# Four more 4 KB tiles in the general pool, and a smaller scratch for dynamic DMAs

## The chip, the core and the metric

The kernel runs on one NeuronCore of a Trainium2 chip. The metric is the device time of one execution in microseconds, lower is better; a run's time covers the profiled span of the core (first to last instruction) and a few microseconds around it.

## What is computed

One layer of an encoder on 2048 tokens of width 1024, all in float32:

```
xn  = rmsnorm(x, norm_mix)
u   = xn @ w_in                       # q 512, k 512, v 1024, o 1024, gates 16
h   = mlstm_scan(q,k,v,gates) forward + the same backward   # 16 chunks of 128 tokens, 4 heads
h   = headnorm(h) * head_norm * sigmoid(o)
x   = x + h @ w_out
x   = x + square(relu(rmsnorm(x, norm_mlp) @ w1)) @ w2      # w1 1024x4096, w2 4096x1024
x   = x + sigmoid(rmsnorm(x, norm_ple) @ ple_gate_w + b) * (p @ ple_w)
out = rmsnorm(x, norm_final)
```

The scan carries a matrix state per head from chunk to chunk, so chunks run in sequence; everything else is matrix products on token blocks.

## The kernel before, in words

Each float32 operand of a product is split into a high part and a remainder, both of a rounded float32 type, and each product of two operands becomes three matmuls (high by high, high by low, low by high; `mm3`, L186 to L189). So in front of TensorE stands a constant stream of splits: ScalarE writes the high part (`A.copy`), VectorE subtracts to get the low part (`split`, L165 to L167). The big projections (k, q and o of the second half of the tokens, w1, w2) are done with a seven-product scheme on 2x2 blocks (`SEVEN`, L418): blocks are added and subtracted first (`sa`, `ta`, `T1` to `T4`), then split (`op`), then multiplied.

The stages, in order of time:

- up to about 270 us: norm of x, the v projection of the second half, then seven-product jobs for k, q and o;
- to about 540 us: v, k, q and o of the first half, with the backward scan woven in (`bwd_steps`, L806: load v and k of a chunk, split them, update the state, store it to `cb_d`);
- to about 900 us: the forward scan over 16 chunks (`Chunk`, L943), with `w_out` and the start of the MLP's input;
- to about 1520 us: the product with w1 for two blocks of tokens (`up_job`, L1264), results stored to `hid_d`;
- to about 2150 us: the product with w2 (`down_job`, L1292); hidden values come back by `hst` loads (L1111, L1116), weights by `wst` loads (L1128), sums go out as accumulating DMAs (L1297);
- to the end: the gate stage, token tile by token tile (`Tok`, L1372). Tokens are transposed by a round trip through memory: `Early_h.put` (L1357) writes eight DMAs of 128 KB each from GpSimd, `Early_h.get` (L1365) reads them back.

**Memory.** Nearly all tiles of the kernel come from one general pool: `Ht` (L74) makes a tile with tag `H`, and all tiles of that tag share `NH` slots, each as large as the largest tile of the tag (4128 bytes a partition for the state tiles with 4 x 258 floats; most tiles are 4096). Staged weights, split weights, transposed tokens, block sums, split operands, hidden values, the scan's tiles: all are `H`. Two smaller pools stand beside it: `O` (`NO` = 7 slots) for loads that are read early, and `S` (6 slots of 2 KB) for results on the way out. The instruction that first writes a tile has to wait until all readers of the slot's last tile are done; if that instruction is a load, the whole DMA queue of SyncE waits behind it, and if it is a split, its engine does.

**Order.** Up to L1504 the order on VectorE, ScalarE and TensorE is the order of the program text (`strict`). After that the framework's planner sets the order of each queue when the program is built: it simulates the kernel with its own costs and lets each engine take the earliest instruction of the program text whose inputs and slot are free at that moment. On the chip the queues then run in that fixed order. So the number of slots enters twice: in waits on the chip, and in the order that the planner writes down.

**DMAs.** SyncE issues most loads and many stores (hardware descriptors); GpSimd issues 408 DMAs whose descriptors are written by software into the scratch for dynamic DMAs, which lies at the bottom of every partition of the on-chip memory, 16384 bytes of it by default. The framework gives the DMAs of GpSimd eight completion counters in turn, so a ninth one waits until the first of the last eight has landed.

The lines that set the sizes:

```
NH = 39
NO = 7
def Ht(name, shape, dt=F32):
    return sb.tile(shape, dt, tag="H", bufs=NH, name=name)
```

Of the kernel before, what the change touches and what calls it, by code (L numbers as in the profile page):

```python
# [26 lines left out]
DFF = 4096  # L27
PLE = 256
EPS = 1e-6
NH = 39  # L30
NO = 7
QC, KC, VC, OC, GC = 0, 512, 1024, 2048, 3072

# [2 lines left out]
def hybrid_mlstm_kernel(  # L36
# [37 lines left out]
    def Ht(name, shape, dt=F32):  # L74

        return sb.tile(shape, dt, tag="H", bufs=NH, name=name)

# [1670 lines left out]
```

## Time and profile before

| | |
|---|---|
| time, median of 3 runs | 2401.54 us (2399.94 to 2401.57) |
| span of the profiled execution | 2396.9 us |
| median of the runs less that span | 4.6 us |
| TensorE busy | 2359.8 us (98%) |
| VectorE, ScalarE, GpSimd busy | 1564.8, 1164.3, 629.9 us |
| DMA | 441.18 MB, mean 184 GB/s |
| largest DMA issues | `wst<-in_mlp_w` 96 of 512 KB, 5.2 us to landing; `h_d<-o` 96 of 512 KB, 13.4 us |

The profile holds one execution. Its own time outside the span is not recorded, so it is compared with the runs through the 4.6 us between span and median. Of the profile's views the following are used: the page, the table of busy time by stretches, who waited for whom, the chain of work, and the time line of one engine.

### The profile page before, as it was taken

The numbers are of one execution on the slowest core, as the hardware profiler recorded it, in microseconds if no ns is written. First come the engines' busy times: TensorE is split into PE (matmuls) and PEld (weight loads), VectorE is DVE, ScalarE is ACT, GpSimd is POOL, SyncE is SP. The second block draws the span as 40 slices with busy tenths as digits, with TensorE's granted clock in tenths as the row PEclk, the third lists the DMA queues.
The fourth block names the chain that finished last, engine by engine and source line by source line (L and its number), as shares of the span: only waits on it lengthen the run. The fifth ranks groups of instructions, "written<-read, shape, count | busy, mean of one in ns | idle before, by whom it ended". The sixth has DMA issues, their size and how long they took to land.

```text
span 2396.9 us, 31578 instructions
## 1 busy us (share of the span) xinstructions
PE 2359.8 (98%) x11221; PEld 1949.9 (81%) x11221; DVE 1564.8 (65%) x2611; ACT 1164.3 (49%) x2166; POOL 629.9 (26%) x679
## 2 busy tenths in 40 slices
PE   7999999999999999999999999999999999999998
PEld 6988888788889887888888888787888888888886
DVE  6677545557778887666685544767666667666665
ACT  5234434437788874343353333444444444455554
POOL 0041122124333324446533332011111111111121
PEclk9999999999999999999999999999999999999999
DMA  5676656868668883456663332568686776796453
GB/s 177 228 225 196 192 144 224 281 220 295 230 227 296 277 269 110 132 169 209 215 228 106 106 114 71 176 134 196 142 189 164 170 170 153 173 216 178 136 138 87
DMA packets 274038, 441.18 MB, mean 184 GB/s; under 512 B 48936, under 2 KB 182440, under 8 KB 273880
## 3 DMA queue, kind: packets, MB, share of 16 engines
q1 hardware_dynamic: 211608, 309.00, 39.3%
q0 software_dynamic: 61984, 129.64, 23.2%
q8 instruction: 88, 1.44, 0.2%
q14 instruction: 70, 0.57, 0.1%
q10 hardware_dynamic: 288, 0.52, 0.1%
HBM read 263.39 MB, written 175.50 MB: 183 GB/s over the span
## 4 chain that ended last, share of the span: by engine, by line
PE 91%; DVE 4%; ACT 2%; issue 1%; DMA 1%; POOL 0%; DVEq 0%; ACTq 0%; SPq 0%; POOLq 0%
PE pa L100 33%; PE pb L100 16%; PE pc L100 8%; PE pg L100 7%; PE psf L100 7%; PE psv L100 7%; PE pso L100 5%; PE pn L100 2%; PE pl L100 2%; PE pu L100 2%; PE pt L100 1%; DVE op L100 1%; PE pS L100 0%; ACT jk L100 0%; DMA wst<-in_mlp_w 0%
## 5 line engine op out<-in xcount | busy, mean ns | idle before, releaser
L100 PE MATMUL pa<-op 128*128 128x512 f32 x3360 | 824.2, 394 | 3.6 <-ACT e L100 2.1
L100 PEld LDWEIGHTS pa<-op 128*128 128x128 f32 x3360 | 629.5, 188 | 155.7 <-ACT e L100 4.4
L100 PE MATMUL pb<-op 128*128 128x512 f32 x1632 | 407.7, 394 | 0.8 <-DVE op L100 0.8
L100 PEld LDWEIGHTS pb<-op 128*128 128x128 f32 x1632 | 306.2, 188 | 73.8 <-DVE op L100 1.1
L100 DVE TENSOR_TENSOR op<-sa,op 128x1024 fp32r<-128x1024 f32 (+2 forms) x176 | 189.1, 1080 | 143.3 <-ACT op L100 109.7
L100 ACT CAST op<-sa 128x1024 fp32r<-128x1024 f32 (+2 forms) x176 | 156.6, 894 | 189.7 <-PE pb L100 98.1
L1297 POOL DMA_DIRECT2D h_d<-o x96 | 94.8, 1033 | 529.9 <-DVE o L100 443.7
L100 ACT COPY e<-pa 128x512 f32<-128x512 f32 x160 | 93.7, 586 | 278.4 <-PE pa L100 277.9
L100 PE MATMUL pc<-op 128*128 128x512 f32 x768 | 191.9, 394 | 0.1
L100 PEld LDWEIGHTS pc<-op 128*128 128x128 f32 x768 | 144.1, 188 | 34.6 <-DVE op L100 0.6
L100 PE MATMUL psv<-whi,xT 128*128 128x272 f32 (+2 forms) x720 | 161.1, 317 | 0.6 <-DVE xT L98 0.6
L100 PE MATMUL psf<-xT,whi 128*128 128x512 f32 x512 | 160.9, 395 | 0.0
L100 ACT CAST op<-wst 128x512 fp32r<-128x512 f32 x112 | 92.5, 834 | 113.9 <-DVE op L100 59.8
L100 DVE TENSOR_TENSOR op<-wst,op 128x512 fp32r<-128x512 f32 x112 | 122.8, 1099 | 30.8 <-ACT op L100 18.5
L467 POOL TENSOR_TENSOR sa<-wst 128x512 f32<-128x512 f32 x32 | 58.8, 1838 | 262.2 <-PE pb L100 167.3
L100 PEld LDWEIGHTS psv<-whi,xT 128*128 128x128 f32 x720 | 118.6, 188 | 9.8 <-DVE xT L98 0.8
L100 PE MATMUL psv<-wlo,xT 128*128 128x272 f32 (+2 forms) x360 | 113.8, 316 | 0.0
L100 PEld LDWEIGHTS psf<-xT,whi 128*128 128x128 f32 x512 | 95.4, 188 | 21.3
L100 DVE TENSOR_TENSOR op<-hst,op 128x384 fp32r<-128x384 f32 (+1 forms) x96 | 65.5, 688 | 64.7 <-ACT op L100 45.1
L100 PE MATMUL pso<-whi,hThi 128*128 128x512 f32 x256 | 102.0, 399 | 2.6 <-ACT nt L100 1.4
L100 PE MATMUL pg<-whi,xTh 128*128 128x512 f32 x256 | 101.4, 397 | 0.0
L100 PE MATMUL psf<-xT,wlo 128*128 128x512 f32 x256 | 100.9, 394 | 0.0
(261 smaller groups left out, 4371.4 us busy)
## 6 DMA issues: line engine op xcount, KB each, us to landing
wst<-in_mlp_w SPq DMA_DIRECT2D x96, 512.0 KB, 5.2
h_d<-o POOLq DMA_DIRECT2D x96, 512.0 KB, 13.4
hid_d<-e SPq DMA_DIRECT2D x128, 256.0 KB, 2.5
hst<-hid_d SPq DMA_DIRECT2D x64, 384.0 KB, 6.8
wst<-in_mlstm_w_in SPq DMA_DIRECT2D x44, 512.0 KB, 5.2
vst<-v_d SPq DMA_DIRECT2D x31, 512.0 KB, 4.7
raw<-in_x SPq DMA_DIRECT2D x16, 512.0 KB, 6.6
kq<-kq_d SPq DMA_DIRECT2D x16, 512.0 KB, 4.0
```

Source lines behind the costliest of these rows:

```text
L100: r = f(*a, **kw)
L467: eng.tensor_tensor(s[:, 0], r1[:, :, P:], r2[:, :, P:], op=add_)
L1297: G.dma_start(rows(h1_d, 2 * q + i), o[i], accum_op=add_)
```

## The change

Two numbers. The pool's slots go from 39 to 43, for all tiles with the tag `H` at once, in every stage; and the scratch for software descriptors goes from the default 16384 to 4096 bytes a partition. Four slots of 4128 bytes are 16512 bytes; 12288 come from the scratch and the rest from bytes that no tile used. No instruction is added or taken out.

```diff
-NH = 39
+NH = 43
 NO = 7
...
-    nc = _bacc.Bacc("TRN2", target_bir_lowering=False, num_devices=1)
+    nc = _bacc.Bacc("TRN2", target_bir_lowering=False, num_devices=1, dynamic_dma_scratch_size=4096)
```

## The prediction, made before the result was known

> **What bounds the kernel now.** First the table of the cores, for the span and the mean granted clock, then the busy time of each engine on the page.
>
> ```profile
> core 0: 2396.9 us, clock 0.997
> ```
>
> ```profile
> PE 2359.8 (98%) x11221; PEld 1949.9 (81%) x11221; DVE 1564.8 (65%) x2611; ACT 1164.3 (49%) x2166; POOL 629.9 (26%) x679
> ```
>
> TensorE is idle for 2396.9 - 2359.8 = 37.1 us of the span, at nearly the full granted clock. More memory removes no matmul, so it can only shorten this idle time. Next, where it lies: the table of busy time by stretches of 60 us (window, PE busy and its count, then PEld, DVE, ACT, POOL, clock, DMA share, GB/s), and below it the first and the last matmul from the time line of TensorE.
>
> ```profile
> 0.00:60.00 60.00, 47.63 (x222) 37.22 (x223) 37.63 (x74) 32.16 (x63) 0.83 (x7) 1.00 0.54 177
> 420.00:480.00 60.00, 57.46 (x272) 47.76 (x271) 33.10 (x77) 24.95 (x43) 11.54 (x18) 0.97 0.86 283
> 540.00:600.00 60.00, 56.78 (x309) 48.07 (x308) 43.49 (x75) 42.16 (x104) 29.11 (x31) 1.00 0.81 291
> 600.00:660.00 60.00, 58.34 (x352) 50.86 (x351) 45.66 (x100) 46.57 (x131) 20.41 (x29) 1.00 0.69 234
> 840.00:900.00 60.00, 58.92 (x330) 50.70 (x328) 48.32 (x90) 44.65 (x114) 14.53 (x17) 1.00 0.79 263
> 900.00:960.00 60.00, 57.92 (x248) 46.21 (x247) 45.59 (x45) 27.07 (x34) 28.55 (x12) 1.00 0.34 110
> 1320.00:1380.00 60.00, 60.00 (x261) 48.58 (x260) 29.28 (x31) 20.25 (x28) 20.52 (x14) 1.00 0.36 114
> 1500.00:1560.00 60.00, 59.06 (x251) 46.53 (x250) 42.89 (x72) 28.62 (x48) 5.99 (x6) 1.00 0.59 183
> 1620.00:1680.00 60.00, 59.17 (x254) 47.29 (x253) 42.89 (x69) 28.28 (x45) 7.29 (x8) 1.00 0.78 188
> ```
>
> ```profile
> 8.65 0.45 PE L100 MATMUL pt<-ident,xs 128*128 128x128 f32 x1 [8.65 <-DVE xs L98]
> ```
>
> ```profile
> 2385.08 0.40 PE L100 MATMUL pl<-whi,pTl 128*128 128x512 f32 x1
> ```
>
> The first stretch lacks 60 - 47.63 = 12.4 us: 8.65 before the first matmul, the rest in the ramp, whose order is fixed by hand and whose pool is still empty. Behind the last matmul stand 2396.9 - 2385.5 = 11.4 us of final norm and stores, which ask for no slot of the pool. That leaves 37.1 - 12.4 - 11.4 = 13.3 us in between. The rows show where: 2.5 at 420 to 480, 3.2 and 1.7 at 540 to 660, 1.1 and 2.1 at 840 to 960, 0.9 at 1500, 0.8 at 1620; the remaining 1.0 is spread over stretches not shown. A middle stretch (1320) is full, with 261 matmuls. So 13.3 us, and what the clock adds, is all that slots can win.
>
> **What a gap costs beside its length.** Two stretches around the gap at 435:
>
> ```profile
> 435.40:438.60 3.20, 0.70 (x3) 0.19 (x1) 1.82 (x6) 2.80 (x7) 0.76 (x1) 1.00 1.04 400
> 438.60:442.00 3.40, 3.36 (x13) 3.24 (x14) 3.40 (x9) 0.84 (x1) 0.00 (x0) 0.50 0.68 200
> ```
>
> TensorE was busy for 0.70 of 3.20 us, and for the next 3.40 us the granted clock is 0.50. At half speed that loses 1.70 us, so this place costs 2.54 + 1.70 = 4.2 us, and the whole that can be won is 13.3 + 1.7 = 15.0 us. Shorter gaps elsewhere show no such drop in the rows above. [...]
>
> **The change, first part: four more slots.** Who waits on TensorE in the middle, and which waits upstream are for a slot:
>
> ```profile
> PE pa L100 <- ACT e L100: 2.1, 2, 1.4
> PE pu L100 <- ACT wk L100: 2.0, 1, 2.0
> PE pu L100 <- ACT nt L100: 1.7, 5, 0.6
> PE pso L100 <- ACT nt L100: 1.4, 1, 1.4
> ...
> PE pn L100 <- DVE vl L100: 0.9, 1, 0.9
> ```
>
> ```profile
> SPq L1128 <- PE pb L100: 7.3, 2, 6.3
> ```
>
> ```profile
> SPq L779 <- DMA cb_d<-Chi: 35.0, 2, 25.8
> ```
>
> ```profile
> POOL sa L467 <- PE pso L100: 22.0, 1, 22.0
> ```
>
> (The first fence is of the whole span; the others are of 1600 to 1640, 240 to 540 and 880 to 935 us.) A load (SPq L1128, L779) that waits for a matmul or for a store to land has no input from these: it waits for the slot that they still read. The pool is thus full in every stage from the scan on, and in steady stages that costs nothing (261 matmuls in 60 us). Only ramps can gain. I go through them.
>
> *At 1620.* The chain of waits shows one gap from slot to matmul:
>
> ```profile
> 1623.70 9.85 DMA wst<-in_mlp_w
> 1633.55 0.02 issue
> 1633.57 0.62 ACT op L100
> 1634.20 0.49 ACT e L100
> 1634.73 1.66 PE pa L100 x6
> ```
>
> A matmul frees the slot (the row of L1128 above), the load of w2 starts, lands 9.85 us later, ScalarE splits it, and only then empties a bank that TensorE needs. With one free slot the load starts earlier and the split is not waited for. Both ramps of the w2 stage lose 0.94 + 0.83 = 1.8 us; from 0 to 1.8, I take 1.0, since only the second is shown to hang on a slot.
>
> *At 900.* GpSimd's first block sum of the next w1 job (L467) sat 22.0 us for a slot that the output projection of the scan held (`pso`). The gaps behind it, 3.2 us with those before 900, end in ScalarE's `e`. From 0 to 3.2, I take 1.5: the sum is then done before VectorE is crowded, but the gap before 900 is not of this kind.
>
> *At 435.* The load of v for the backward scan waits on stores of the state in this stage (25.8 us in its longest case). In the gap itself ScalarE's cast of v stood behind an emptying of a bank, which is order, not a slot; an earlier load lets the planner place the cast ahead. From 0 to 4.2, I take the middle, 2.1.
>
> *At 540 to 660.* 4.9 us, with VectorE 43 to 46 and ScalarE 42 to 47 of 60 us busy; the releasers are `nt` and `vl`, casts and copies that stand in a queue behind other work. From 0 to 4.9, I take 1.0, nearest to the rows of full queues.
>
> Sum: 1.0 + 1.5 + 2.1 + 1.0 = 5.6 us. The upper bound is 15.0. Below nothing it is bounded by the planner: it writes a new order wherever a slot comes free earlier in its simulation, and an order that its costs misjudge makes a gap like that at 435, 4.2 us each. I take one sum, -5.6, and keep +4.2 to +8.4 (one or two such gaps) for the range. Work is not lengthened: loads come earlier, and the DMA share is 0.34 to 0.86 in the stretches shown.
>
> **Second part: the smaller scratch.** The cost is a wait of GpSimd for room. What bounds it is how many of its DMAs are in flight; the time line of GpSimd in the last stage, the line of its writes and that of the reads back (count, first and last start, time to landing), and the last piece of matmuls on the chain:
>
> ```profile
> 2334.07 0.69 POOL L1433 DMA_DIRECT2D out<-h  x1 [10.48 <-DVE h L100]
> 2335.95 4.53 POOL L1362 DMA_DIRECT2D h_d<-y  x7 [1.19 <-DVE rst L100]
> 2345.46 0.65 POOL L1362 DMA_DIRECT2D h_d<-y  x1 [4.99 <-DMA out<-h]
> ```
>
> ```profile
> L1362 POOL DMA_DIRECT2D h_d<-y x48: 648/651/694, 2179.6 to 2345.5; - x48
> ...
> DMA to landing us min/median/max: 2.7/4.5/9.6
> ```
>
> ```profile
> L1369 SPq DMA_DIRECT2D z<-h_d x12: 355/361/392, 2186.9 to 2350.1; - x12
> ...
> DMA to landing us min/median/max: 7.1/9.3/11.6
> ```
>
> ```profile
> 2361.82 22.28 PE pg L100 x96
> ```
>
> The program itself lets eight be in flight: the eighth write of a burst waits 4.99 us until the `out` store, eight issues back, has landed. So a smaller ring costs nothing as long as it holds eight of these writes, the ones with the most pieces (512 runs of 256 bytes by L1362 and L1363). Is there cover if it does not? The last read back is issued at 2350.1 and takes up to 11.6 us, to 2361.7, and the matmuls that use it begin at 2361.82: the last burst has none. Bounds: 0, and one more wait of 5.0 us in each of 48 / 8 = 6 bursts, 30 us; a gain is excluded, since nothing gets shorter. I take 0: the rows show eight in flight as the most, and the first of the seven, issued at 2335.95, lands 9.6 us later at most, at 2345.6, about when the eighth is issued.
>
> By the Trainium skill ("DMA: Bandwidth & Descriptors", section "Terms") a descriptor has 16 bytes and GpSimd's are written to rings in this memory; with its one closing descriptor a write would need 512 / 16 + 1 = 33 per engine, and 4096 / 16 = 256 hold seven, not eight. By that, an estimate, the eighth would wait only until the first of the seven lands. No run here shows the ring's size.
>
> **The sum against the profiled execution.** 2396.9 - 5.6 + 0 = 2391.3 us of span. Median and span differ by 2401.54 - 2396.9 = 4.6 us, so 2395.9 us as a run's time, 0.23% less. About 0.2% (4.8 us) is what a measurement of this kernel can tell from no change.
>
> **The rivals.**
>
> *Nothing changes (2401.5).* For it: 98% busy, most slot waits lie in stretches with full TensorE, and the gaps at 540 to 660 end in busy engines. Against it: the 9.85 us load on the chain at 1623 and the 22.0 us at 900 are waits for slots.
>
> *All of the middle goes (2386.5).* 2401.5 - 15.0. For it: casts in the scan's ramp also need slots. Against it: 840 to 900 and 540 to 660 have gaps whose releaser is an engine at 42 to 48 of 60 us.
>
> *A worse order (2405.7).* One mechanism: ScalarE's queue. Where a slot frees earlier, the planner puts a cast of a late load ahead of the emptying of a bank, as at 1633, where `e` stood behind `op`. If that falls where VectorE and ScalarE are fullest, 540 to 660, TensorE stops for some 2.5 us and the clock halves, 4.2 us. It decides from the point where such gaps exceed the 5.6 won; with nothing won and one gap, 2401.5 + 4.2 = 2405.7. For it: four of the gaps above end in a cast or copy of ScalarE. Against it: steady stages have banks enough to run without a gap.
>
> *The ring is too small (2411.5).* GpSimd stops within a burst of eight and the read back comes late. It decides where the ring holds clearly fewer than eight of these writes: the last two bursts, with little or no cover, pay 5.0 us each, 10 us in all. For it: the missing cover at 2361.8. Against it: the first write lands about when the eighth is issued, so a ring for seven hardly waits.
>
> **How the numbers follow.** Forecast 0.44, between 2388 and 2400, four fifths of it below 2396.7; nothing 0.28; all goes 0.06; worse order 0.15; ring 0.07. Faster by over 0.2%: 0.36 + 0.06 = 0.42. Within: 0.08 + 0.28 + 0.02 of the worse order = 0.38. Slower: 0.13 + 0.07 = 0.20. The range from 2387 to 2407 leaves out the ring, a part of the worse order with two gaps, and the half of the full gain, about 0.15.
>
> **What would show it.** Right: matmuls in 60 us at 1620, 900 and 420 near the full count; L467's wait at 900 shorter; the load of w2 gone from the chain at 1623; no half clock at 438; the eighth write of a burst still released by the landing of a store, with 5 us. Wrong: the same gaps with the same releasers (slots were not the cause), new gaps behind ScalarE with a clock of 0.5 (order), or waits inside the first seven writes of a burst (ring).

## The result, and the profile after

| | before | after |
|---|---|---|
| median of the runs | 2401.56 us (2399.94 to 2407.35) | 2425.57 us (2423.89 to 2429.8) |
| span of the profiled execution | 2396.9 us | 2423.7 us |

The changed kernel takes 1.0097 of the time before (95% interval 1.0086 to 1.0109). It is 24 us slower, where 5.6 us less were forecast, and lies outside the predicted range. The two profiled executions differ by 26.8 us; where the time went is worked out against that number.

By its page, TensorE is busy for 2367.2 us after, 98% of the span as before, with the same 11221 matmuls, and no engine has more instructions. The loss shows only by stretches. Of the kernel before, three rows that the prediction did not show (window, PE busy and its count, PEld, DVE, ACT, POOL, clock, DMA share, GB/s):

```profile
720.00:780.00 60.00, 60.00 (x385) 54.20 (x385) 48.06 (x99) 51.15 (x141) 21.37 (x27) 1.00 0.85 292
780.00:840.00 60.00, 60.00 (x377) 53.83 (x376) 49.23 (x103) 51.22 (x141) 20.94 (x30) 1.00 0.86 284
1200.00:1260.00 60.00, 59.76 (x259) 48.15 (x258) 49.18 (x46) 33.10 (x43) 23.39 (x13) 1.00 0.70 228
```

and of the changed kernel:

```profile
600.00:660.00 60.00, 56.46 (x335) 50.38 (x336) 44.28 (x92) 44.36 (x122) 22.56 (x31) 0.94 0.65 220
...
720.00:780.00 60.00, 57.08 (x336) 49.63 (x335) 46.06 (x93) 46.60 (x128) 18.02 (x26) 1.00 0.76 267
780.00:840.00 60.00, 55.79 (x348) 49.05 (x347) 45.05 (x91) 48.88 (x130) 22.00 (x29) 1.00 0.66 234
...
900.00:960.00 60.00, 56.44 (x246) 44.98 (x244) 58.28 (x61) 35.71 (x56) 24.15 (x10) 1.00 0.52 170
1200.00:1260.00 60.00, 56.75 (x241) 45.39 (x240) 45.06 (x42) 31.13 (x40) 19.42 (x11) 0.98 0.70 222
1500.00:1560.00 60.00, 60.00 (x261) 48.55 (x260) 35.97 (x51) 23.34 (x37) 6.46 (x4) 1.00 0.36 118
1620.00:1680.00 60.00, 56.64 (x237) 45.12 (x236) 39.74 (x61) 26.66 (x43) 9.12 (x9) 0.97 0.68 155
```

Read the counts of matmuls, since they also hold what a lower clock costs. In the scan, 720 to 840, TensorE was full and now does 684 matmuls instead of 762. The groups of the output projection (`pso`) tell when the scan ends (before, then after; the last two numbers ahead of the form are the first and last start):

```profile
L100 PE MATMUL pso<-whi,hThi x256: 387/394/505, 587.0 to 906.0; 128*128 128x512 f32 x128
```

```profile
L100 PE MATMUL pso<-whi,hThi x256: 387/394/505, 588.0 to 923.4; 128*128 128x512 f32 x128
```

The scan ends 17.4 us later. The other 9.4 us come behind it: at 1200 to 1260 there are 18 matmuls fewer, at 60 / 261 = 0.23 us each 4.1 us; at 1620 to 1680 17 fewer, 3.9 us; at 1500 to 1560 10 more, 2.3 us won. The remaining 3.7 us are small gaps further on from the scan, mostly behind VectorE by the view of waits: 9 matmuls fewer at 960 to 1020 and 7 fewer at 1080 to 1140.

**The scan.** The order of SyncE's queue in the scan is the same as before; only the times are different. Line L954 loads kq of a chunk (its keys and queries), L956 mb and L958 ib (tables made from the gates, 512 KB each), and L968 the state for the backward direction, in two loads of 516 KB: Chi, then Clo. Before:

```profile
L954 SPq DMA_DIRECT2D kq<-kq_d x6: 393/402/424, 740.9 to 845.7; - x6
```

```profile
L968 POOL DMA_DIRECT2D Chi<-cb_d x4: 580/580/580, 748.4 to 811.3; - x4
```

```profile
POOL Chi L968 <- PE pso L100: 36.8, 4, 9.2
```

After:

```profile
L954 SPq DMA_DIRECT2D kq<-kq_d x5: 375/403/426, 746.9 to 839.6; - x5
```

```profile
L968 POOL DMA_DIRECT2D Chi<-cb_d x4: 574/576/583, 745.3 to 814.4; - x4
L968 POOL DMA_DIRECT2D Clo<-cb_d x4: 528/536/543, 747.9 to 817.0; - x4
```

A chunk took (845.7 - 740.9) / 5 = 20.96 us and takes (839.6 - 746.9) / 4 = 23.2 us. By the starts of kq in the time line, the six chunks from 720 on take 137.9 us instead of 125.9: that is 12.0 of the 17.4 us. Of the other 5.4, 3.9 are lost ahead of these chunks; 600 to 660 has 17 matmuls fewer. What follows explains the 12.0.

Before, Chi waited some 9 us per chunk for a slot that matmuls of the output projection still read, and started 7.5 us behind kq (748.4 against 740.9), with Clo 0.6 us behind it. Now its slot is free and it starts 1.6 us ahead of kq. That is what the slots were to do. Clo still waits, 2.05 us by the time line of GpSimd, and starts 1.1 us behind kq. The load of mb follows kq by 0.5 us: so 0.5 MB of the state is now ahead of mb and the other 0.5 MB 0.6 us behind it, where before all of it came 7 us later. ScalarE cannot go on without mb. The landing time of mb in the scan, from the view of that tile from 600 to 850 us, before and after:

```profile
DMA to landing us min/median/max: 4.9/5.9/6.7
```

```profile
DMA to landing us min/median/max: 4.4/7.9/10.7
```

The chain of waits after shows a loop through that load, once per chunk:

```profile
747.36 10.78 DMA mb<-nm_d
...
758.23 0.33 ACT mb L100
...
762.17 2.54 POOL ib L988 x2
...
764.73 1.05 ACT qsh L100
...
766.87 0.98 ACT zt L100 x2
...
768.16 0.09 SPq L1191
...
770.66 10.43 DMA mb<-nm_d
```

mb lands after 10.78 us, and ScalarE takes its exponentials. GpSimd masks them (L998, at 760.12 and 761.55 in its time line) and then, in its order, forms `ib` (L988); ScalarE splits that (`qsh`) and comes, in its order, to the copies `nt` and `zt`. SyncE's store L1191 waits for `zt`, and behind the store in the same queue stand the loads of the next chunk, mb among them: 23.3 us from one mb to the next. Before, the chain in this stretch was matmuls alone. The DMA engines are full while mb is under way, in both kernels (before, then after):

```profile
741.40:752.20 10.80, 10.80 (x64) 9.47 (x64) 7.98 (x17) 8.26 (x28) 1.67 (x3) 1.00 1.02 357
```

```profile
747.40:758.10 10.70, 10.17 (x57) 8.62 (x56) 7.89 (x16) 5.89 (x19) 0.53 (x1) 1.00 1.02 363
```

So no load was added; who comes first in a full burst was changed.

**Behind the scan.** The time line of ScalarE, and of TensorE, near 1254 after:

```profile
1255.55 1.56 ACT L100 CAST op<-wst 128x512 fp32r<-128x512 f32 x2 [6.11 <-DVE op L100]
1257.02 0.58 ACT L100 COPY e<-pb 128x512 f32<-128x512 f32 x1
```

```profile
1257.65 4.52 PE L100 MATMUL pb<-op 128*128 128x512 f32 x12 [3.25 <-ACT e L100]
```

and of ScalarE at the same place of the job before:

```profile
1231.44 0.58 ACT L100 COPY e<-pb 128x512 f32<-128x512 f32 x1
...
1240.37 1.57 ACT L100 CAST op<-wst 128x512 fp32r<-128x512 f32 x2 [3.46 <-DVE op L100]
```

Before, the emptying of the bank (`e<-pb`) stood ahead of the casts of `wst`, and their wait for VectorE cost nothing. With more slots the planner places those casts ahead of the emptying; on the chip they wait 6.11 us for VectorE, the emptying behind them is late, and TensorE stops for 3.25 us. (The input of the casts is a load. So what they wait for is most likely a slot that VectorE still reads; the trace names the releaser only.) The granted clock then falls:

```profile
1257.40:1260.80 3.40, 3.15 (x7) 2.48 (x8) 3.29 (x3) 0.20 (x1) 0.92 (x1) 0.51 0.85 286
```

At 1652 the chain of waits after has the load of w2 that the prediction wanted gone:

```profile
1641.30 12.17 DMA wst<-in_mlp_w
...
1653.55 0.63 ACT op L100
1654.18 0.68 DVE op L100
1654.86 0.61 DVE o L100
...
1655.52 5.31 PE pa L100 x15
```

ScalarE's cast waits 3.89 us for the load (by its time line). VectorE's half of the same split stands ahead of its emptying of a bank (`o`), and TensorE waits 3.14 us for that.

### The profile page after: what moved, and what is told of

The parts are those of the page before. It is cut to its first block, busy times and chain, and to the rows that moved or that the text cites. A ratio compares the mean times of both kernels' runs of the same rounds, so it can differ in the third digit from the quotient of the medians.

```text
span 2423.7 us, 31524 instructions
## 1 busy us (share of the span) xinstructions
PE 2367.2 (98%) x11221; PEld 1955.9 (81%) x11221; DVE 1570.2 (65%) x2611; ACT 1165.3 (48%) x2166; POOL 621.1 (26%) x679
## 4 chain that ended last, share of the span: by engine, by line
PE 82%; DVE 6%; DMA 5%; ACT 3%; issue 2%; SPq 1%; POOL 1%; DVEq 0%; ACTq 0%; POOLq 0%
PE pa L100 31%; PE pb L100 15%; PE pc L100 8%; PE pg L100 7%; PE psv L100 7%; PE psf L100 6%; DMA mb<-nm_d 3%; PE pso L100 2%; PE pl L100 2%; PE pu L100 2%; DVE op L100 1%; PE pn L100 1%; DMA wst<-in_mlp_w 1%; ACT nt L100 1%; DVE e L100 1%
## 5 line engine op out<-in xcount | busy, mean ns | idle before, releaser
L1297 POOL DMA_DIRECT2D h_d<-o x96 | 94.7, 999 | 550.2 <-DVE o L100 418.7
L472 POOL TENSOR_TENSOR sa<-wst 128x512 f32<-128x512 f32 x32 | 46.9, 1465 | 215.5 <-PE pb L100 190.4
L100 PE MATMUL pso<-whi,hTlo 128*128 128x512 f32 x256 | 100.6, 394 | 0.0
```

Of the source, the lines that this page charges most:

```text
L100: r = f(*a, **kw)
L472: eng2.tensor_tensor(s[1][:, 0], r1[:, :, :P], r1[:, :, P:], op=sub_)
L1297: G.dma_start(rows(h1_d, 2 * q + i), o[i], accum_op=add_)
```

## The experiments

Each time stands beside runs of the kernel before on the same chip (2401.2 to 2402.0 us).

**The two halves of the change, and fewer slots.** The scratch alone (39 slots):

```diff
-    nc = _bacc.Bacc("TRN2", target_bir_lowering=False, num_devices=1)
+    nc = _bacc.Bacc("TRN2", target_bir_lowering=False, num_devices=1, dynamic_dma_scratch_size=4096)
```

> The kernel before (39 slots) with the smaller scratch alone; the order of every queue stays that of the kernel before. Theory 'slots' (the 24 us come from the four slots): no change, 2401.5 us, within 2. Rival 'ring' (the smaller scratch delays GpSimd's DMAs, and the slower scan and the gaps are what that looks like): most of the 24 us, above 2415.

2401.24 us, ratio 0.9998 (0.9988 to 1.0007). So the slots are the cause. (43 slots with the scratch of 16384 bytes do not fit, so the two halves are not taken apart at 43.) Then `NH = 40` with the default scratch, and `NH = 41` with 4096 bytes:

> One slot more (40) with the default scratch, for which there is just room. Theory 'slots': a part of the loss already here, some 3 to 8 us over 2401.5, by a longer period of the scan's chunks or by one new gap of order. Rival 'ring': no loss, 2401.5 or a little less.

> Two slots more (41) with the scratch of 4096 bytes. Theory 'slots': between 40 and 43 slots, some 2405 to 2418 us; if the loss hangs on one particular load that needs a slot, a step rather than a slope. Rival 'ring': as with 43 slots, about 2425, since the scratch is the same.

2406.27 us (ratio 1.0020, 1.0011 to 1.0029) and 2409.84 us (1.0028, 1.0016 to 1.0039): a slope. Where these lose is not the scan from 720 on: its period stays 21.0 us in both. By the tables of stretches they lose around 600 us and by late gaps. In the time line the state load starts 6.6 us behind kq with 40 slots and 3.9 us with 41, so mb is still ahead of it. The load of v (L779) starts 1.4 to 2.1 us behind kq with 41 slots, as early as with 43 (1.5 to 2.3; 6.3 with 39), and the period is 21.0 us all the same: the early load of v is not what makes a chunk longer.

**Loads set apart.** In the changed kernel one slot for v and two for the state, 40 for the rest:

```diff
-NH = 43
+NH = 40
...
-            self.v = v_load(c)
+            self.v = v_load(c, Vt)
...
-                self.cb = [Ht(nm, [P, H, DVX], F32R) for nm in ("Chi", "Clo")]
+                self.cb = [Cbt(nm, [P, H, DVX], F32R) for nm in ("Chi", "Clo")]
```

(`Vt` makes tiles of a tag with one buffer, `Cbt` of a tag with two; `v_load` takes the maker of its tile as an argument. Both are used in the forward scan alone.)

> The changed kernel with the same memory, but three of the 43 slots are set apart in the scan: one for the load of v (L779), two for the load of the backward state (L968), so that these loads wait again for the last chunk's readers. Theory 'collision' (the early loads of v and of the state run beside the load of mb, which lands 10.4 instead of some 6 us after its issue, and the chunk's loop closes through it): the period goes from 23 back to 21.0 us, and 12 to 14 of the 24 us come back, some 2411 to 2414 us. Rival 'order' (new gaps of the planner's order alone): still 2425. Rival 'ring': still 2425.

2412.40 us (1.0045, 1.0030 to 1.0060). The number came as the theory said, the way did not: in the later chunks the period is still 22.3 us. The last reader of the state is an earlier instruction than the one that had freed the old slot, so the loads of the state start even sooner, 5.4 to 3.2 us ahead of kq. What came back is the first half of the scan and most of the gaps at 1254 and 1652 (254 and 250 matmuls in their stretches). The run is no proof of the theory, but points at the state loads, since v was late again (6 to 8 us behind kq) and the period long.

So the state alone, with all else as before (39 slots, two more for Chi and Clo, scratch 4096):

> The kernel before (39 slots for everything else, scratch of 4096 bytes) with two slots more for the backward state alone (L968), so that its loads can start as soon as the products of the chunk before are done; nothing else gets a slot. Theory 'collision, by the state loads': they start 1.5 to 5 us ahead of kq, the period of the later chunks goes from 21.0 to 22 or 23 us, and the time rises by 6 to 12 us, to 2408 to 2414 us. Rival 'it takes the fuller queue of all loads' (v too): no change, 2401.5 us.

2412.40 us (1.0045, 1.0030 to 1.0060). The views of L957 (kq) and L971 (Chi) of this kernel:

```profile
L957 SPq DMA_DIRECT2D kq<-kq_d x5: 500/945/1109, 745.4 to 834.1; - x5
```

```profile
L971 POOL DMA_DIRECT2D Chi<-cb_d x5: 586/586/595, 740.0 to 830.7; - x5
```

The state starts 5.4 to 3.1 us ahead of kq, and a chunk takes (834.1 - 745.4) / 4 = 22.2 us. Two slots in the wrong hands cost 11 us by themselves.

The same kernel also shows what else it takes. Chunks whose kq is loaded at 618 to 700 us have no store by L1191 yet; the first starts at 719 us. There Chi starts 2.1 us and Clo 1.5 us ahead of kq by the time line, mb lands after 6.0 to 7.3 us, and a chunk takes 20.6 us, less than before. The DMA share is 0.66 from 610 to 718 us and 0.77 from 718 to 850. So there an early state load costs nothing. It costs in the chunks that have the store; there the burst is fuller as well, and the two are not told apart.

**Move the loads in the queues instead.** All at 43 slots. First the state loads on SyncE:

```diff
-                    G.dma_start(self.cb[i], cb_d[c, :, i].bitcast(F32R))
+                    SP.dma_start(self.cb[i].bitcast(F32), cb_d[c, :, i])
```

> The changed kernel (43 slots), with the two loads of the backward state (L968) issued by SyncE instead of GpSimd, so that they stand in one queue behind kq, mb and ib, and behind the store of the chunk's sum (L1083). Theory 'collision, by the state loads' (the two 0.5 MB loads are issued 1.5 us ahead of kq and mb, and mb queues behind them): mb lands in some 6 to 7 us again, the period of the chunks is 21.0 us, and 10 to 13 us come back: 2412 to 2415 us. Rival 'the early v load does it', or 'order': the period stays 23, 2425 us.

2456.71 us (1.0231, 1.0216 to 1.0247), a miss of 40 us. By the time line, behind the store L1083, which waits for VectorE, the state starts 9.3 to 10.8 us behind kq, in later chunks 14.7 us, and Clo later still; everything behind it in SyncE's queue is held up as well, and a chunk takes 24.6 us, the last ones 26.0. The expectation had overlooked that wait. Whether the late state or the held-up queue costs this is not told apart here; in the next run a state 12 us behind kq costs nothing.

Then mb alone, on GpSimd, where it stands ahead of the state:

```diff
-            SP.dma_start(self.mb, nm_d[c].partition_broadcast(P))
+            G.dma_start(self.mb, nm_d[c].partition_broadcast(P))
```

> The changed kernel (43 slots), with the load of mb (L956) issued by GpSimd, where it stands ahead of the state loads (L968) and no longer behind SyncE's store of the normed tokens (L1191). Theory 'collision': mb no longer queues behind the state loads, the period goes back to 21.0 us, and 10 to 14 us come back: 2411 to 2415 us. Rival 'the chain of the chunk is long for another reason': 2425 us or more, with mb landing early and the period still 23.

2414.04 us (1.0058, 1.0041 to 1.0075), as the collision says. Its loads of mb:

```profile
L956 POOL DMA_DIRECT2D mb<-nm_d x6: 568/568/571, 744.4 to 849.2; - x6
```

(849.2 - 744.4) / 5 = 21.0 us per chunk; mb starts 1.3 us ahead of kq, the state some 12 us behind it. And the store that closes the loop, on GpSimd:

```diff
-                SP.dma_start(x0_d[t // 4, :, :, sl].rearrange("k p t -> p k t"), z)
+                G.dma_start(x0_d[t // 4, :, :, sl].rearrange("k p t -> p k t"), z)
```

> The changed kernel (43 slots), with the store of the normed tokens (L1191), which waits for ScalarE's last copy of the chunk, issued by GpSimd instead of SyncE, so that kq, mb and ib no longer stand behind that wait, and the state loads (L968) do. Theory 'collision, closed to a loop by that store': kq and mb are issued earlier, ahead of the state loads, the period is 21.0 us again in the chunks that have the store (from 720 to 880 us), and 10 to 13 us come back: 2412 to 2415 us. Rival 'other reason': 2425 us or more.

2415.77 us (1.0065, 1.0050 to 1.0081). From 765 on:

```profile
L954 SPq DMA_DIRECT2D kq<-kq_d x4: 319/320/320, 765.4 to 828.3; - x4
```

The state now starts 4.2 us behind kq, and the period is (828.3 - 765.4) / 3 = 21.0 us. Both moves also take mb from behind the store L1191, so they show that the late mb and the loop together cost the 2 us per chunk, and not what either costs alone. The kernels side by side, in the chunks that have the store:

| kernel | Chi starts, against kq (us) | us per chunk |
|---|---|---|
| 39 slots | +7.5 | 21.0 |
| 40, 41 slots | +6.6, +3.9 | 21.0 |
| 43 slots, store on GpSimd | +4.2 | 21.0 |
| 43 slots | -1.6 | 23.2 |
| 39 and two for the state | -5.4 to -3.1 | 22.2 |
| 40, two for the state, one for v | -5.4 to -3.2 | 22.3 |
| 43 slots, mb on GpSimd at -1.3 | +12.2 | 21.0 |
| 43 slots, state on SyncE | +9.3 to +14.7 | 24.6 |

(Starts from the time line of the later chunks, 740 to 850 us.) On GpSimd, the period is 21.0 us wherever Chi starts 3.9 us or more behind kq, and longer wherever it starts ahead; how far ahead does not set how much longer.

**Which half of the kernel.** Four of the 43 slots are held by tiles that nobody uses, until the scan's end or from there on. The first two tries held nothing:

> The changed kernel, with four of its 43 slots held by tiles that nobody uses (two GpSimd instructions of one element each) from the start to the end of the scan: 39 slots up to about 900 us, 43 after. Theory 'two causes' (16 us are lost in the scan, the rest by gaps of order behind it): 2425.5 - 16 = 2409 us, within 4, the gaps near 934, 1254 and 1652 us still there. Rival 'one cause' (the late gaps follow from the scan): 2401.5 us.

> The complement: 43 slots up to the end of the scan, then four held until the gate stage, so 39 for the two products of the MLP. Theory 'two causes': 2401.5 + 16 = 2417 us, within 4, the gaps near 1254 and 1652 us gone. Rival 'one cause': 2425 us.

2429.52 and 2426.03 us. The instruction that gives the slots back had no input but the held tile, so the planner put it right behind the one that takes them. These two are the changed kernel once more, and say nothing of the theories. But the first one has its first matmul at 13.45 us instead of 8.74, since the tiles at the start reordered the first loads, and it takes 4.0 us more than the changed kernel (2425.57): most of a late start reaches the end. The second try makes the last reader depend on late data:

```diff
+    def keep(t, dep): held.append(t); (G.memset(t[0:1, 0:1], 0.0) if dep is None else G.tensor_copy(t[0:1, 0:1], dep))
+    def hold(n, dep=None): [keep(Ht("hold", [P, D]), dep) for _ in range(n)]
+    def free(dep): [G.tensor_tensor(t[0:1, 1:2], t[0:1, 0:1], dep, op=ALU.add) for t in held]
...
+    free(l.vx[1][0:1, 0, 0:1].bitcast(F32))
```

(In the first kernel `hold(4)` stands at the start. In the complement `hold(4, l.vx[1][0:1, 0, 0:1].bitcast(F32))` stands in place of the last line, and `free` ahead of the gate stage.)

> The changed kernel, with four of its 43 slots held from the start until the last v split of the scan has been read (the instruction that gives them back now depends on that tile): 39 slots up to about 880 us, 43 after. The order of SyncE's queue up to there is that of the kernel before. Theory 'two causes': the scan's 16 us come back, the gaps behind it stay: 2425.5 - 16 = 2409 us, within 3. Rival 'one cause' (the late gaps follow from the late scan): 2401.5 us.

> The complement, held from the last v split of the scan until the gate stage's first tokens are split: 43 slots up to about 880 us, 39 in both products of the MLP. Theory 'two causes': 2401.5 + 16 = 2417 us, within 3; the chunks' period is 23 us, the gaps at 1254 and 1652 are gone. Rival 'one cause': 2425 us.

39 slots in the scan: 2413.58 us (1.0050, 1.0032 to 1.0068). 39 slots behind it: 2417.71 us (1.0071, 1.0056 to 1.0086). Of the first:

```profile
13.63 0.45 PE L100 MATMUL pt<-ident,xs 128*128 128x128 f32 x1 [13.63 <-DVE xs L98]
```

```profile
780.00:840.00 60.00, 60.00 (x373) 53.65 (x373) 49.92 (x104) 51.18 (x139) 21.64 (x29) 1.00 0.83 276
1200.00:1260.00 60.00, 56.74 (x238) 45.46 (x237) 46.63 (x44) 31.16 (x40) 21.14 (x12) 0.97 0.70 224
```

of the second:

```profile
1200.00:1260.00 60.00, 60.00 (x259) 48.27 (x259) 48.47 (x45) 32.56 (x41) 23.39 (x14) 1.00 0.63 209
...
1620.00:1680.00 60.00, 58.94 (x253) 47.08 (x252) 43.61 (x68) 30.04 (x47) 10.04 (x10) 1.00 0.76 177
```

In the first the scan is full and the gap at 1254 is there. In the second the gaps at 1254 and 1652 are gone, and its chunks take 23.4 to 24.5 us by the time line. The causes are two. The first kernel, at 2413.58, is above the 2409 within 3 that were expected, and far from the rival's 2401.5. It also starts 5.0 us later (13.63 against 8.65), like the try that held nothing, where that came to 4.0 us. Less 4.0 to 5.0 it would be at 2408.6 to 2409.6, where it was expected; that is an estimate. Both cures together (mb on GpSimd, four slots held behind the scan):

> Both cures at 43 slots: mb loaded by GpSimd ahead of the state loads, and four slots held during the products of the MLP. Theory 'two causes, and they add': of the 24 us the first gives back 11.5 (2425.6 to 2414.0) and the second 7.9 (2425.6 to 2417.7), so 2406 us, within 3. Rival 'they overlap': above 2411 us.

2404.93 us (1.0011, 1.0002 to 1.0020): of the 24 us, 20.6 go when both causes are taken away. The causes add. The 3.5 us that are left stay open.

**A test that turned into another.** The state's own two slots with 39 others, and mb on GpSimd:

> 39 slots and two more for the state loads alone, as in the run that took 2412.4 us, and mb loaded by GpSimd ahead of them. Theory 'collision with mb': the period is 21.0 us again and the time that of the kernel before, 2401.5 us, within 3. Rival 'early state loads cost by themselves' (they take the memory's time from others): still 2409 to 2412 us.

2421.20 us (1.0081, 1.0066 to 1.0095), and neither theory's number. From the chain of waits:

```profile
773.27 11.88 DMA ib<-in_d
```

By the same chain Chi is issued at 769.49 and mb at 773.10: with slots of its own the state stands ahead of mb on GpSimd too, and mb and ib both come behind it; now ib is late with 11.88 us. So the theory was not tested as meant. Whether early state loads cost anything in these chunks with mb and ib ahead of them is not shown: at 43 slots with mb on GpSimd they are not early.

**Slots at a ramp alone.** By the trace the four slots are held from 347 to 1458 us and from 1547 to 2157:

> 43 slots only around the start of the product with w2: four are held from about 400 us to about 1460 and again from about 1570 to the gate stage. Theory 'a slot is worth something only at a ramp': the 2.1 us that TensorE loses at 1500 to 1560 go, nothing else changes, 2399.5 us. Rival 'the order pays it back' (a new gap of 2 to 4 us where the planner packs splits earlier): 2401 to 2404 us.

2401.16 us, ratio 1.0000 (0.9991 to 1.0010).

```profile
1500.00:1560.00 60.00, 60.00 (x260) 48.53 (x259) 45.04 (x74) 28.47 (x48) 4.43 (x8) 0.95 0.62 184
```

The ramp at 1500 is full now, with 9 matmuls more than before. Against that, 1440 to 1500 has 5 fewer, and 300 to 360 a gap of 0.8 us that was not there. What is left is below what can be told; 2399.5 us of the theory and the 2401 of the rival lie too near each other to choose. None of the kernels run here is faster than the kernel before.

**How near the scratch was.** With 4096 bytes alone, the last two bursts of GpSimd's writes look different from before, though nothing is slower:

```profile
2336.28 3.90 POOL L1362 DMA_DIRECT2D h_d<-y  x6 [1.19 <-DVE rst L100]
2345.89 1.29 POOL L1362 DMA_DIRECT2D h_d<-y  x2 [5.72 <-issue]
```

Six writes go, and the seventh waits 5.72 us for nothing that the profile shows; before, seven went and the eighth waited 4.99 us for a store. So 2048 bytes, with the order of before:

> The kernel before (39 slots) with a scratch of 2048 bytes, half of the changed kernel's; the order of every queue is that of the kernel before. Theory 'the wait inside a burst is room in the scratch': it comes earlier in the burst, after two or three writes instead of six, and more than once; in the last two bursts the last write starts some 5 us later than before (2345.5), so that the read back, which had no cover there, makes TensorE wait: 2404 to 2412 us. Rival 'that wait is something else' (the profile only fails to show the counter): the burst looks as with 4096 bytes and the time is 2401.5 us.

2691.10 us (1.1201, 1.1174 to 1.1229), some 280 us more than expected. In the last burst of writes the waits come as the theory says, early and more than once: after the first write, after the second (8.03 us), and twice more. GpSimd's waits with no releaser ahead of L1297, with 4096 bytes and 39 slots, and with 2048 (2.9 us in all with the default):

```profile
POOL h_d L1297 <- issue: 24.3, 7, 10.4
```

```profile
POOL h_d L1297 <- issue: 443.8, 32, 18.9
```

The wait inside a burst is room in the scratch. But the price falls in another place than the bursts: the accumulating stores of the product with w2 (L1297) go one at a time, VectorE waits 216 us in all for their landing before it can empty into their tiles, and TensorE 153 us for VectorE. Between 4096 and 2048 bytes lie 290 us.

## Why the prediction was wrong

**The step that failed** is the sentence that closed the first part: "Work is not lengthened: loads come earlier, and the DMA share is 0.34 to 0.86 in the stretches shown." The shares were means over 60 us. Inside a chunk the DMA engines are full (1.02 for 10.8 us, before as after), and a load that comes earlier there takes the place of another. The wait of `POOL Chi` for `PE pso` was idle time off the critical path, and still of use: it kept the 1 MB of the state 7 us behind mb. With 43 slots Chi passes mb and Clo follows it by 0.6 us, mb lands after 10.4 to 10.8 us instead of 5 to 7, and the store L1191 passes the delay on to the next chunk. That explains 12.0 of the 17.4 us of the scan: moving mb ahead, moving the store, and taking the slots from the scan each bring the period back to 21 us, and giving slots to the state alone makes it 22.2. The 5.4 us ahead of and behind these chunks are not explained. This case was in none of the rivals.

**The worse order** came, at 0.15, with its mechanism and nearly its price: a split ahead of the emptying of a bank, 4.2 us forecast for a gap with the halved clock, 4.1 and 3.9 us measured. At 1254 it is ScalarE's cast, as foreseen; at 1652 it is VectorE's half of the split, behind a late load. Its place was wrong. The prediction looked for it where VectorE and ScalarE are fullest and held that "steady stages have banks enough to run without a gap"; it fell into a steady stage, at 1254, where those engines are busy for 45 and 31 of 60 us, and into the ramp at 1652. A full queue is not what is needed for it, only one split that waits ahead of one emptying. That the new order is to blame is read from the time lines; what holds the split up is on the chip a wait for a slot or a load, and no run has the one without the other.

**The gains, term by term.** At 1620, forecast 1.0 won: 3.9 lost; the load of w2 is on the chain again, lands in 12.17 us instead of 9.85, and SyncE waits for its slot as before. At 900, forecast 1.5: GpSimd's wait for the scan's slot is hardly shorter,

```profile
POOL sa L467 <- PE pso L100: 20.5, 1, 20.5
```

(22.0 before): the pool is full there again, and 900 to 960 has 246 matmuls instead of 248. At 435, forecast 2.1: the same gap to 0.03 us and nearly the same half clock,

```profile
435.30:438.50 3.20, 0.67 (x3) 0.19 (x1) 1.85 (x6) 2.83 (x7) 0.76 (x1) 0.97 1.04 410
438.50:441.90 3.40, 3.39 (x14) 3.25 (x15) 3.40 (x9) 0.81 (x1) 0.00 (x0) 0.53 1.09 356
```

so that gap did not hang on the number of slots. At 540 to 660, forecast 1.0: 17 matmuls fewer at 600 to 660. Only the ramp at 1500 gave what its row said. No run came near the upper bound of 15.0 us; the lower bound, one or two gaps, failed, since it counted the planner's order and not the loads.

**The scratch** was right in its cost, 0, and not in its reason. Not eight but six writes and a store are in flight, and the last one starts 1 us later. The page cited from the Trainium skill ("DMA: Bandwidth & Descriptors", section "Terms") had led to an estimate of seven, which is nearer to the six and a store than the eight of the prediction. The seventh write of a burst did wait, 5.72 us, and nothing came of it. The bound of 30 us looked at the wrong instruction: with half that scratch the loss is 290 us, and the stores by L1297 make it.

## What to carry to other kernels

A buffer that comes free late is also a throttle: before adding slots, list the loads that wait for one, and ask ahead of which load in the same burst they will then stand, in windows as short as the burst and not as long as a stage. Ask also what waits for the load that is passed, and whether that hands the delay to the next round. If order is written by a planner, slots given to all stages change the order of all of them; give them to one stage and look at the others' matmul counts. And when a resource is made smaller for room, run it once at half the new size: it shows which instruction lives on it and how far the edge is.

## What the runs showed that was not expected

The same gap in the starting ramp, 1.8 us of TensorE between 32 and 38 us, is followed by a lower clock in some profiled executions and not in others, with the same order of TensorE's matmuls up to there. The changed kernel, and the try that was to hold slots behind the scan and held none:

```profile
38.00:44.00 6.00, 6.00 (x39) 5.03 (x38) 5.60 (x10) 4.75 (x8) 0.00 (x0) 1.00 0.46 133
```

```profile
38.00:44.00 6.00, 6.00 (x21) 4.92 (x19) 4.30 (x7) 2.81 (x5) 0.00 (x0) 0.54 0.42 126
```

39 matmuls against 21 in 6 us: at a clock of 0.54, 6 x 0.46 = 2.8 us, and no difference between the kernels accounts for it. The Trainium skill ("TensorE: Matmul & The Clock Gate", section "What's actually happening") says that the window by which the clock is set runs freely and does not start anew with the kernel, so that the point of a change depends on where in it the first matmul falls. These rows would fit that, but no run here shows the window.

A granted clock of 0.95 in the records need not cost anything: the profiled execution of the kernel with slots at the ramp shows it for most of its span, with 260 matmuls in 60 us, as many as others do at 1.00. It took 2401.16 us, the median of that kernel; the ten other executions, at 0.995 to 0.998, took 2398.47 to 2406.28.
